# Seven products in both last MLP chunks, masks added by VectorE, and another order of the first loads

## The chip, the core and the metric

The kernel runs on one core of a Trainium2 chip. The metric is the device time of one execution in microseconds (us). Before the change the median of three runs is 2133.43 us (2133.31 to 2133.77). The trace that is read below is that of one more, profiled execution of the same kernel.

Engines by their names in the trace: PE is TensorE (PEld its weight loads), DVE is VectorE, ACT is ScalarE, POOL is GpSimd, SP is SyncE. SPq, ACTq and POOLq are the queues on which these issue DMAs. PSUM holds matmul results, SBUF everything else.

## The reference

Two decoder layers on x of 256 tokens by 2048 features, all in float32:

```python
for i in range(2):
    h = rms_norm(x, norm_mix[i])
    x = x + (nsa_mixer if i == 0 else gla_mixer)(h, ...)
    h = rms_norm(x, norm_mlp[i])
    x = x + jnp.square(jax.nn.relu(h @ w_up)) @ w_down      # 2048 -> 8192 -> 2048
```

`nsa_mixer` is attention with 16 query heads over 4 key groups and three branches (16 compressed keys, selected blocks, a window). With 256 tokens the selected blocks and the window cover all earlier keys, so two of the branches are causal attention over 256 keys. Scores that are not allowed are replaced by -1e30 before the softmax. `gla_mixer` is gated linear attention with 4 heads; the causal part within a sequence is computed by levels of halving blocks.

## The kernel before

**Arithmetic.** Each float32 operand of a large matmul is split into a high part of type fp32r (ACT casts it: tile `wh` for weights) and the rest (DVE subtracts: `wl`). A product is three matmuls: high by high, high by low, low by high. A matmul streams 512 columns against a 128x128 stationary tile. `a_half` consumes one weight half (128x1024: two k tiles of 512 columns) with 12 matmuls, six for each block `t` of 128 tokens.

**Stages in time.** NSA projections and attention (to about 270 us), NSA output projection (to 395), MLP of layer 0 (to about 1058), GLA (to about 1417 with its output projection after it), MLP of layer 1 (to the end).

**The MLP.** The hidden dimension is cut into 8 chunks of 1024. Chunk `c` computes hidden activations of `c + 1` (items `U`, 16 matmuls each) between the items of its own down product. In chunks 0 to 6 the down product of 256 tokens by 1024 hidden by 1024 output columns is done by a seven-product scheme (two groups a chunk, items `S`; a product is 12 matmuls of 512 columns). Sums of weight blocks that it needs are made by DVE or by accumulating DMAs on POOL's queue; sums of activation blocks (seven planes instead of four) by DVE in `hidden`. Chunk 7 (`SEVENS[7]` = 0) is plain: 16 items `C`, each one `a_half`.

**The order of the work** is written out by `Plan`: it adds up assumed costs for PE, ACT and DVE while the program is generated. Side work (attention heads, the GLA exponents, the norms) are generators, `streams`, that yield the time at which their next step is ready; `tick`, called every few matmuls, steps those that are ready. Engines then run their instruction lists in order. What a step is assumed to cost therefore decides where its instructions stand, not how long they take.

**Start.** SP issues the norm gains (`cid`, columns 128 on), then four quarters of the first two weight units, x's second pair of feature tiles, two halves, one unit of 1 MB, then x's third and fourth pair. ACT's queue loads x's first pair. Six idle products (12 entries in the trace) run on PE until data are there.

**GLA, first head.** `exponents` (four streams, one a head, one after the other) builds the decay factors: copies from `laT` and `rest`, additions, two tiles `g` of 8 levels a head. `attn` multiplies them with keys and queries (`g<-g,kq`), makes score blocks (`psx<-g`), transposes three of them (`psx<-cid,g`), places them with 20 predicated copies into `att` (line 1747), and splits `att` into `ath`. `head_out` multiplies `ath` with the values (`psx<-g,ath`).

**NSA scores.** `attend` (line 1331) makes the scores of one head in PSUM. The mask is added by a matmul of an identity with the mask (`maskr`, `identr`), twice a head; DVE takes row maxima (`reduce`), ACT exponentiates from PSUM.

Of the kernel before, what the change touches and what calls it, by code (L numbers as in the profile page):

```python
# [10 lines left out]
F32 = mybir.dt.float32  # L11
# [18 lines left out]
SEVENS = (2, 2, 2, 2, 2, 2, 2, 0)  # L30
# [3 lines left out]
class Plan:  # L34
# [49 lines left out]
    def spawn(self, gen):  # L84
        s = {"gen": gen, "ready": 0.0, "need": {}, "done": False}
        self.streams.append(s)
        self._step(s)
        return s
# [9 lines left out]
    def tick(self, slack=3200.0):  # L98
        taken = set()
        for s in list(self.streams):  # L100
# [8 lines left out]
    def drain(self, s, enough=lambda: False):  # L109
        while not s["done"] and not enough():  # L110
            before = [(id(q), q["ready"], q["need"]) for q in self.streams]
            self.tick(1e9)
# [3 lines left out]
    def wait(self, needs):  # L116

        while not all(sum(f < 1e12 for f in self.slots[tag]) >= n for tag, n in needs.items()):
            self.tick(1e9)
# [4 lines left out]
def trunk_kernel(ctx: ExitStack, tc: tile.TileContext, a: dict, out: bass.AP):  # L124
# [159 lines left out]
    nc.sync.dma_start(cid[:, P:], a["cid"][:, P:])  # L284
# [7 lines left out]
    nc.scalar.dma_start(xpair[0], a["x"][0])  # L292
    nc.gpsimd.memset(mhalf, -0.5)
# [62 lines left out]
    class Weights:  # L356
# [46 lines left out]
        def load_first(self, between):  # L403
# [4 lines left out]
            for j, (i, lo, hi) in enumerate(((0, 0, 512), (0, 512, 1024), (1, 0, 512), (1, 512, 1024), (0, 1024, 2048), (1, 1024, 2048))):  # L408
                nc.sync.dma_start(self.raws[i][:, lo:hi], self.units[i][0][:, lo:hi])  # L409
# [119 lines left out]
    MIXES = {0: "C" * 16, 2: "UU" + "SUSUSUSUSUUSUS" + "SUSUSUSUSUUSUS"}  # L529

    def mlp_items(c):
        return MIXES[SEVENS[c]]

    def mlp_units(layer):
# [8 lines left out]
        for c in range(8):  # L543
            down = a["mlp_down"][layer, c]
            n = {"U": 0, "S": 0, "C": 0}
            for it in mlp_items(c):
                i = n[it]
                n[it] += 1
                if it == "S":
                    if i % 7 == 0:  # L550
                        g = weights.group([down[i // 7, u] for u in range(4)])
# [5 lines left out]
                else:  # L557
                    if i % 2 == 0:
                        uc = weights.unit(down[SEVENS[c] + i // 8, i // 2 % 4])
# [184 lines left out]
    class PrepTokens(Prep):  # L744
# [3 lines left out]
        def start(self, b):  # L748
            if b == 0:
# [37 lines left out]
    def mlp(prep, after, last):  # L787
        op = prep.op
        with tc.tile_pool(name="mlpz", bufs=1) as zp:
# [20 lines left out]
            class Up:  # L810


                def __init__(self, c):
                    self.c = c
                    self.pairs = []
                    self.zz = None
                    self.pss = {}

                def half(self, f, half):
# [10 lines left out]
                    if f % 2 == 0:  # L830
                        self.pairs.append(pair_tile(c, f // 2))
                    last_z[:] = [W.spawn(self.hidden(ps, f))]

                def hidden(self, ps, f):
# [17 lines left out]
                    n = 7 if "S" in mlp_items(self.c) else 4  # L852
                    if n == 7:
                        both = pz[:, 0, :]
                        both = bass.AP(tensor=both.tensor, offset=both.offset,
                                       ap=[list(both.ap[0]), [3 * P, 2], [1, P]])
# [3 lines left out]
                    ht = self.pairs[f // 2][0]  # L860
# [18 lines left out]
            class Seven:  # L879
# [4 lines left out]
                def __init__(self, pairs, b):  # L884
# [4 lines left out]
                def product(self, name):  # L889
# [31 lines left out]
            class Plain:  # L921


                def __init__(self, c, pairs, first):
                    self.c, self.pairs, self.first = c, pairs, first
# [1079 lines left out]
```

## Time and profile before

| | |
|---|---|
| median of 3 runs | 2133.43 us |
| the profiled execution: its time, its span | 2133.26 us, 2131.5 us |
| TensorE clock granted, mean over the span | 0.999 of full speed |
| PE busy | 2121.5 us (100%), 10971 matmuls |
| DVE busy | 1784.3 us (84%) |
| ACT busy | 1358.4 us (64%) |
| DMA | 482.20 MB, mean 226 GB/s |

A busy time counts an instruction from its start to its modelled end. Matmuls overlap, so the mean duration of a 512 column matmul in the page (393 ns) is not its price; the distance from one start to the next is. A time in a timeline is the start, from the span's beginning; the number after it is the time that the merged instructions cover; in square brackets stands the idle time of the engine before them and what ended it.

### The profile page before, as it was taken

Reading aid. Unit: us, or ns where it says so; the run is one execution under the profiler, and the core shown is the slowest. Engines: PE = TensorE matmul, PEld = TensorE weight load, DVE = VectorE, ACT = ScalarE, POOL = GpSimd, SP = SyncE. Lnnn points to the kernel's source line nnn. Section 1 sums busy time; section 2 is a strip of 40 time slices with the busy share of each in tenths; the row PEclk is TensorE's granted clock in tenths of the full one; section 3 lists DMA queues with packets and bytes.
Section 4 is the critical chain, followed back from the end, with each engine's and each line's share of the span. In section 5 each row is a group of like instructions: output and inputs, shape, how many; then the busy total and the mean of one; then the engine's idle time right before and its main releaser. Section 6 shows DMA issues by size and latency. Waiting matters only on the chain.

```text
span 2131.5 us, 29821 instructions
## 1 busy us (share of the span) xinstructions
PE 2121.5 (100%) x10971; PEld 1797.3 (84%) x10971; DVE 1784.3 (84%) x2626; ACT 1358.4 (64%) x2047; POOL 154.9 (7%) x184
## 2 busy tenths in 40 slices
PE   9999999999999999999999999999999999999999
PEld 7888888888888888888888788888888888888887
DVE  7778777789999999998658987667899999999985
ACT  6568676666667666666566564536666666667663
POOL 0010100000110011001000000000000100010010
PEclk9999999999999999999999999999999999999999
DMA  7554444769889879878645354556698898798784
GB/s 287 205 198 139 153 164 149 235 227 297 257 241 299 265 243 281 274 240 244 203 162 194 130 176 173 174 187 238 225 300 258 238 291 268 244 279 278 240 240 153
DMA packets 97826, 482.20 MB, mean 226 GB/s; under 512 B 12176, under 2 KB 12832, under 8 KB 64144
## 3 DMA queue, kind: packets, MB, share of 16 engines
q1 hardware_dynamic: 76320, 403.53, 52.2%
q0 software_dynamic: 21216, 76.51, 18.0%
q8 instruction: 86, 1.41, 0.2%
q14 instruction: 60, 0.49, 0.1%
q10 hardware_dynamic: 144, 0.26, 0.0%
HBM read 404.76 MB, written 2.10 MB: 191 GB/s over the span
## 4 chain that ended last, share of the span: by engine, by line
PE 98%; DVE 1%; DMA 0%; issue 0%; ACT 0%; SPq 0%; ACTq 0%
PE psa L166 59%; PE psx L166 37%; PE psx L170 2%; DVE wl L201 0%; DVE g L201 0%; DMA raw<-in_nsa_in_dram 0%; DVE att L1747 0%; DVE g L1599 0%; DVE laT L201 0%; DVE rest L201 0%; DVE g L205 0%; ACT wh L197 0%; DVE xt L205 0%; DVE ath L201 0%; SPq L409 0%
## 5 line engine op out<-in xcount | busy, mean ns | idle before, releaser
L166 PE MATMUL psa<-wh,op 128*128 128x512 f32 x2616 | 849.7, 393 | 0.2 <-ACT wh L197 0.2
L201 DVE TENSOR_TENSOR wl<-raw,wh 128x1024 fp32r<-128x1024 f32 (+1 forms) x530 | 643.1, 1218 | 182.3 <-ACT wh L197 171.3
L197 ACT CAST wh<-raw 128x1024 fp32r<-128x1024 f32 (+1 forms) x534 | 557.5, 1046 | 291.8 <-PE psa L166 260.5
L166 PEld LDWEIGHTS psa<-wh,op 128*128 128x128 f32 x2616 | 492.4, 188 | 102.6 <-ACT wh L197 0.6
L201 DVE TENSOR_TENSOR wl<-sraw,wh 128x1024 fp32r<-128x1024 f32 x392 | 473.5, 1220 | 52.4 <-ACT wh L197 47.3
L166 PE MATMUL psx<-op,wh 128*128 128x512 f32 (+1 forms) x2080 | 515.8, 390 | 0.0
L166 PE MATMUL psa<-wl,op 128*128 128x512 f32 x1308 | 511.2, 391 | 0.2 <-DVE wl L201 0.2
L197 ACT CAST wh<-sraw 128x1024 fp32r<-128x1024 f32 x392 | 412.2, 1053 | 152.4 <-PE psa L166 59.5
L166 PEld LDWEIGHTS psx<-op,wh 128*128 128x128 f32 (+1 forms) x2080 | 385.1, 188 | 77.8
L166 PE MATMUL psa<-wh,ht 128*128 128x512 f32 x1128 | 382.0, 391 | 0.0
L166 PEld LDWEIGHTS psx<-op,wl 128*128 128x128 f32 x2048 | 279.5, 191 | 20.0
L166 PEld LDWEIGHTS psa<-wl,op 128*128 128x128 f32 x1308 | 246.3, 188 | 48.5 <-DVE wl L201 0.8
L166 PE MATMUL psx<-op,wl 128*128 128x256 f32 x2048 | 286.2, 283 | 0.0
L166 PEld LDWEIGHTS psa<-wh,ht 128*128 128x128 f32 x1128 | 212.8, 189 | 39.0
L166 PE MATMUL psa<-wl,ht 128*128 128x512 f32 x564 | 221.7, 393 | 0.0
L338 POOL DMA_DIRECT2D sraw<-sraw x140 | 119.8, 920 | 1289.5 <-DVE pz L201 429.9
L205 DVE SCALAR_TENSOR_TENSOR xt<-psa,r,xt 128x512 f32<-128x512 f32 x212 | 157.4, 745 | 26.9 <-PE psa L166 26.1
L197 ACT COPY zz<-psx 128x256 f32<-128x256 f32 x128 | 47.6, 372 | 169.0 <-PE psx L166 168.8
L166 PEld LDWEIGHTS psa<-wl,ht 128*128 128x128 f32 x564 | 106.7, 189 | 15.3 <-DVE wl L201 0.4
L201 DVE TENSOR_TENSOR sraw<-sraw,sraw 128x1024 f32<-128x1024 f32 x84 | 102.6, 1221 | 1.0
L201 DVE TENSOR_TENSOR zz<-psx,zz 128x256 f32<-128x256 f32 x128 | 53.7, 419 | 13.6 <-ACT zz L197 13.6
L197 ACT CAST ht<-pz 128x896 fp32r<-128x896 f32 (+1 forms) x40 | 37.1, 928 | 14.6 <-DVE pz L205 13.5
(195 smaller groups left out, 1195.8 us busy)
## 6 DMA issues: line engine op xcount, KB each, us to landing
raw<-in_mlp_up_dram SPq DMA_DIRECT2D x128, 1024.0 KB, 7.5
sraw<-in_mlp_down_dram SPq DMA_DIRECT2D x224, 512.0 KB, 11.4
sraw<-sraw POOLq DMA_DIRECT2D x140, 512.0 KB, 9.5
raw<-in_gla_in_dram SPq DMA_DIRECT2D x48, 1024.0 KB, 4.9
raw<-in_nsa_in_dram SPq DMA_DIRECT2D x38, 1024.0 KB, 4.8
raw<-in_nsa_out_dram SPq DMA_DIRECT2D x16, 1024.0 KB, 4.8
raw<-in_mlp_down_dram SPq DMA_DIRECT2D x16, 1024.0 KB, 4.9
raw<-in_gla_out_dram SPq DMA_DIRECT2D x16, 1024.0 KB, 4.8
```

The lines of the kernel that those rows point to most:

```text
L166: nc.tensor.matmul(dst, lhsT, rhs, skip_group_check=True, **kw)
L170: nc.tensor.transpose(dst, src, idn)
L197: nc.scalar.copy(dst, src)
L201: nc.vector.tensor_tensor(dst, x, y, op=op)
L205: nc.vector.scalar_tensor_tensor(dst, x, s, y, op0=op0, op1=op1)
L338: nc.gpsimd.dma_start(dst, src, accum_op=ALU.add)
```

## The change

Five things are edited.

1. `SEVENS` becomes a table for both layers, with 1 for chunk 7: half of its output columns (blocks 2 and 3) by seven products, half (blocks 0 and 1) plain, in the order `CCSCSCSCSCSCSCS`. Plain products need a plane that the seven-product planes overwrite, so `hidden` first stores it apart (`over`). Block results are finished by `finished`: output DMA in layer 1, the start of the next norm (`after.start`) in layer 0.
2. The masks leave PE. DVE adds them while it takes the maxima (`least`, one fused instruction with a second one that reads out its accumulator), writes the masked scores to SBUF, and ACT exponentiates from there.
3. First loads: the gains go to ACT's queue behind x's first pair; SP starts with the weights; x's third pair goes ahead of the 1 MB unit. The first two units lie contiguous in DRAM by piece.
4. `Plan`: the streams `exponents` are marked `later`, stepped after all others and not beyond the slack while another is drained.
5. `Plan`: assumed costs; a GLA copy of 128 elements is reckoned by another, lower formula (`vcopy` in place of `keep`), a predicated copy by 235 in place of 110.

```diff
-SEVENS = (2, 2, 2, 2, 2, 2, 2, 0)
+SEVENS = ((2, 2, 2, 2, 2, 2, 2, 1), (2, 2, 2, 2, 2, 2, 2, 1))
...
-    def tick(self, slack=3200.0):
+    def tick(self, slack=3200.0, later=True):
         taken = set()
-        for s in list(self.streams):
+        for s in sorted(self.streams, key=lambda s: s["later"]):
+            if s["later"] and not later:
+                return
...
+    def least(dst, x, y, acc):
+
+        W.run("dve", free(dst) * 1.042 + 150, [dst, acc], [x, y])
+        nc.vector.tensor_tensor_reduce(dst, x, y, scale=-1.0, scalar=3e38, op0=ALU.add, op1=ALU.min, accum_out=acc)
...
-    nc.sync.dma_start(cid[:, P:], a["cid"][:, P:])
...
     nc.scalar.dma_start(xpair[0], a["x"][0])
+    nc.scalar.dma_start(cid[:, P:], a["cid"][:, P:])
...
-                nc.sync.dma_start(self.raws[i][:, lo:hi], self.units[i][0][:, lo:hi])
+
+                flat = self.units[i][0].rearrange("p n -> (p n)")
+                nc.sync.dma_start(self.raws[i][:, lo:hi], flat[P * lo:P * hi].rearrange("(p c) -> p c", p=P))
...
+    MIXES = {0: "C" * 16, 1: "CCSCSCSCSCSCSCS", 2: "UU" + "SUSUSUSUSUUSUS" + "SUSUSUSUSUUSUS"}
...
                     if i % 7 == 0:
-                        g = weights.group([down[i // 7, u] for u in range(4)])
+                        g = weights.group([down[2 - SEVENS[layer][c] + i // 7, u] for u in range(4)])
+                        if c == 7:
+                            g.odd = 1
...
+                    ht, over = self.pairs[f // 2][0], self.over[f // 2] if self.over else None
+                    if over is not None:
+
+                        copy(over[:, 0, :], pz[:, 1, :])
+                        yield W.ready(over)
+                        tt(over[:, 1, :], pz[:, 1, :], over[:, 0, :].bitcast(F32), ALU.subtract)
...
+                        if self.c == 7 and name in ("b21", "t2", "d2", "t4"):
+                            finished(t, b + k)
...
+            def finished(t, b):
+                if last:
+                    nc.sync.dma_start(out[t * P:(t + 1) * P, b * 512:(b + 1) * 512], xt[t][b])
+                elif t == 1:
+                    after.start(b)
...
-                    if mask is not None:
-                        mm(dst, cst["identr"], mask, start=False, stop=False)
...
-                largest(nb0[:, 0:1], s0[:, 256:272])
-                largest(nb0[:, 1:3], s0[:, 0:256].rearrange("p (b k) -> p b k", b=2))
+                masked(nb0[:, 0:1], 0, s0[:, 256:272], mask[:, 272:288])
+                for b in range(2):
+                    masked(nb0[:, 1 + b:2 + b], 32 + b * P, s0[:, b * P:(b + 1) * P], mask[:, 16:16 + P])
+                W.give(s0, W.t["dve"])
...
-                        keep(second, uv[:, :, 1, :])
+                        vcopy(second, uv[:, :, 1, :])
...
-                        W.run("dve", 110.0, [att], [pl])
+                        W.run("dve", 235.0, [att], [pl])
...
-                        sums = sums + [W.spawn(exponents(hd, sums[-1], es[hd]))]
+                        sums = sums + [W.spawn(exponents(hd, sums[-1], es[hd]), True)]
...
     weights.load_first(lambda j: load_x(({}, {0: 3900.0}, {}, {1: 8300.0}, {}, {})[j]))
+    load_x({2: 11200.0})
     weights.load()
-    load_x({2: 13000.0, 3: 13700.0})
+    load_x({3: 13700.0})
```

Three places in the instruction lists. The first is ACT's list at the start. `xs` are x's pairs (the one that has the lowest number came first), `raw_107` and `raw_108` the first two weight units, `raw_116` or `raw_117` the third. Before:

```order
L193 ACTIVATE op_142<-xs_88,cid 128x256 x2
L197 CAST wh_172<-raw_107 128x1024
L197 CAST wh_186<-raw_108 128x1024
L193 ACTIVATE op_197<-xs_89,cid 128x256 x2
L193 ACTIVATE op_197<-xs_90,cid 128x256 x2
L193 ACTIVATE psx_209<-xs_87 128x256
L197 CAST wh_217<-raw_116 128x1024
```

After:

```order
L198 ACTIVATE op_142<-xs_87,cid 128x256 x2
L202 CAST wh_172<-raw_107 128x1024
L198 ACTIVATE op_178<-xs_88,cid 128x256 x2
L202 CAST wh_190<-raw_108 128x1024
L198 ACTIVATE op_178<-xs_89,cid 128x256 x2
L198 ACTIVATE psx_211<-xs_86 128x256
L202 CAST wh_218<-raw_117 128x1024
```

The third pair (`xs_89`, now `xs_88`) is scaled one weight cast earlier; on DVE its first remainder now stands directly ahead of the remainder of `wh_172` (`wl_173`), where it stood behind two of these.

The second place is DVE's list in GLA, from the remainder of the first head's `ath` to the first multiplications of the second head (`g<-g,kq`). Before:

```order
L201 TENSOR_TENSOR wl_11391<-raw_11189,wh_11390 128x1024
L201 TENSOR_TENSOR ath_11405<-att_11113,ath_11405 128x384
L205 SCALAR_TENSOR_TENSOR g_2058_11411<-g_2058_11411,psa_11130 128x512
L205 SCALAR_TENSOR_TENSOR g_2058_11411<-g_2058_11411,psa_11131 128x512
L201 TENSOR_TENSOR g_2001_10890<-g_2001_10890,kq_10126 128x256 x4
L1611 MEMSET rest_10123 128x256
```

After:

```order
L206 TENSOR_TENSOR wl_11291<-raw_11096,wh_11290 128x1024
L221 COPY g_2040_11176<-laT 128x128
L221 COPY g_2040_11176<-rest_10149 128x128
L206 TENSOR_TENSOR laT<-g_2040_11176,laT 128x4x32
L206 TENSOR_TENSOR rest_10149<-g_2040_11176 128x4x32
L206 TENSOR_TENSOR ath_11311<-att_11067,ath_11311 128x384
L206 TENSOR_TENSOR wl_11318<-raw_11096,wh_11317 128x1024
L221 COPY g_2040_11176<-laT 128x128
L221 COPY g_2040_11176<-rest_10149 128x128
L206 TENSOR_TENSOR laT<-g_2040_11176,laT 128x2x64
```

The second head's multiplications stood three rows behind `ath`; now they begin 20 rows behind it. On PE 24 matmuls of weights stood between the first head's `psx<-g,ath` and the second head's score blocks, and now 75 do; between the transposes for `att` and `psx<-g,ath` there were 42 and now are 66.

The third place is DVE's list at the first attention head. `psx` are scores in PSUM, `p` the tile that is exponentiated, `nb` the negated maxima. Before:

```order
L201 TENSOR_TENSOR wl_1611<-raw_1466,wh_1610 128x1024
L220 TENSOR_REDUCE nb_305_1636<-psx_1629 128x1
L220 TENSOR_REDUCE nb_305_1636<-psx_1629 128x2
L220 TENSOR_REDUCE nb_311_1648<-psx_1641 128x1
L220 TENSOR_REDUCE nb_311_1648<-psx_1641 128x2
L212 TENSOR_SCALAR f_1568<-f_1568,r2d 128x4 x2
```

After:

```order
L206 TENSOR_TENSOR wl_1571<-raw_1413,wh_1570 128x1024
L230 ISA p_1595,nb_294_1600<-psx_1594,mask 128x16
L230 ISA nb_294_1600 128x1
L230 ISA p_1595,nb_294_1600<-psx_1594,mask 128x128
L230 ISA nb_294_1600 128x1
L230 ISA p_1595,nb_294_1600<-psx_1594,mask 128x128
```

Two reductions of the first score block of a head become three fused instructions, each with a read-out. Over all 16 heads 64 reductions go and 96 fused instructions come (32 of 16 columns, 64 of 128 columns).

## Rows read from the trace of the kernel before

**Rows 1.** The page's part 1: busy us (share of span) x instructions.

```profile
PE 2121.5 (100%) x10971; PEld 1797.3 (84%) x10971; DVE 1784.3 (84%) x2626; ACT 1358.4 (64%) x2047; POOL 154.9 (7%) x184
```

**Rows 2.** Chain of waits in order of time: start, us, what; plain chunk 7, layer 0.

```profile
1030.84 10.90 PE psa L166 x48
```

**Rows 3.** Timeline of PE inside one head's scores.

```profile
185.65 0.29 PE L166 MATMUL psx<-maskr,identr 128*128 128x272 f32 x1
185.78 0.29 PE L166 MATMUL psx<-kT,qT 128*128 128x272 f32 x1
```

**Rows 4.** Timeline of all engines, first 15 us.

```profile
0.74 0.39 SPq L284 DMA_DIRECT2D cid<-in_cid_dram  x1
...
1.19 1.84 SPq L409 DMA_DIRECT2D raw<-in_nsa_in_dram  x4
...
8.12 0.50 PE L166 MATMUL psa<-wl,op 128*128 128x512 f32 x1 [0.22 <-DVE wl L201]
...
11.16 1.06 ACT L197 CAST wh<-raw 128x1024 fp32r<-128x1024 f32 x1 [0.20 <-DMA raw<-in_nsa_in_dram]
...
13.04 0.39 PE L166 MATMUL psa<-wl,op 128*128 128x512 f32 x1
...
14.23 1.71 ACT L193 ACTIVATE op<-xs,cid 128x256 fp32r<-128x256 f32 x4 [2.02 <-DMA xs<-in_x_dram]
```

**Rows 5.** Timeline of PE in GLA, first and second head.

```profile
1196.44 0.58 PE L170 MATMUL psx<-cid,g 128*128 128x128 f32 x3
...
1206.61 0.62 PE L166 MATMUL psx<-g,ath 128*128 128x512 f32 x2
1209.95 2.44 PE L166 MATMUL psx<-g,ath 128*128 128x512 f32 x7 [2.73 <-DVE ath L201]
...
1214.89 0.39 PE L166 MATMUL psa<-wl,op 128*128 128x512 f32 x1
...
1220.98 1.65 PE L166 MATMUL psx<-g 128*32 128x64 f32 x68 [0.64 <-DVE g L201]
...
1223.98 0.33 PE L170 MATMUL psx<-cid,g 128*128 128x128 f32 x1 [0.46 <-DVE g L205]
1224.64 0.55 PE L170 MATMUL psx<-cid,g 128*128 128x128 f32 x3 [0.33 <-DVE g L205]
```

**Rows 6.** Windows: stretch, us, busy us of each engine, granted clock (PEclk), DMA share.

```profile
1210.00:1215.00 5.00, 5.00 (x15) 3.97 (x16) 4.96 (x21) 1.38 (x4) 0.00 (x0) 0.66 0.31 131
...
160.00:340.00 180.00, 180.00 (x962) 153.88 (x961) 138.29 (x337) 135.86 (x463) 13.60 (x12) 1.00 0.44 152
```

**Rows 7.** Tile `att`, 1195 to 1210 us: ns min/median/max, first and last start.

```profile
L1747 DVE COPY_PREDICATED att<-lmask,psx x20: 176/199/234, 1198.9 to 1203.4; 64x32 f32<-64x32 uint8 x20
```

**Rows 8.** Timeline of DVE in GLA, first head's end.

```profile
1206.12 1.23 DVE L201 TENSOR_TENSOR wl<-raw,wh 128x1024 fp32r<-128x1024 f32 x1
1207.26 0.23 DVE L1599 COPY g<-laT 128x128 f32<-128x128 f32 x1
...
1207.93 0.23 DVE L1599 COPY g<-laT 128x128 f32<-128x128 f32 x1
...
1209.34 0.56 DVE L201 TENSOR_TENSOR ath<-att,ath 128x384 fp32r<-128x384 f32 x1
1209.93 1.28 DVE L205 SCALAR_TENSOR_TENSOR g<-g,psa 128x512 f32<-128x512 f32 x2
1211.13 1.43 DVE L201 TENSOR_TENSOR g<-g,kq 128x256 f32<-128x256 f32 x4
```

**Rows 9.** Groups by line, DVE, 160 to 340 us: form, count, busy us, mean ns, idle before.

```profile
L220 DVE TENSOR_REDUCE mx<-psx 128x2 f32<-128x256 f32 x32 | 11.9, 414 | 0.0
L220 DVE TENSOR_REDUCE nb<-psx 128x1 f32<-128x16 f32 x32 | 5.4, 170 | 12.9 <-PE psx L166 12.9
```

**Rows 10.** Timeline of DVE: the fused multiply-and-sum that GLA uses.

```profile
1122.73 0.42 DVE L1661 CUSTOM_DVE_ANT_0 dj<-g,g 128x256 f32<-128x256 f32 x1
...
1123.19 0.43 DVE L1661 CUSTOM_DVE_ANT_0 dj<-g,g 128x256 f32<-128x256 f32 x1
```

More of the change, by code (lines that the diff above doesn't have):

```diff
@@ L545, in mlp_units @@
             n = {"U": 0, "S": 0, "C": 0}
-            for it in mlp_items(c):
+            for it in mlp_items(layer, c):
                 i = n[it]
@@ L558, in mlp_units @@
                     if i % 2 == 0:
-                        uc = weights.unit(down[SEVENS[c] + i // 8, i // 2 % 4])
+                        uc = weights.unit(down[i // 8, i // 2 % 4])
                     weights.half(uc, i % 2)
@@ L788, in mlp @@
         op = prep.op
+        layer = int(last)
+        sevens = SEVENS[layer]
         with tc.tile_pool(name="mlpz", bufs=1) as zp:
@@ L815, in __init__ @@
                     self.pairs = []
+                    self.over = []
                     self.zz = None
@@ L943, in half @@
                         W.give(self.ps[t], W.t["dve"])
-                    if self.c < 7:
-                        return
-                    if last:
+                    if self.c == 7:
                         for t in range(NT):
-                            nc.sync.dma_start(out[t * P:(t + 1) * P, b * 512:(b + 1) * 512], xt[t][b])
-                    if after is not None:
-                        after.start(b)
+                            finished(t, b)
+            def finished(t, b):
[3 more added lines that the diff above has]
+                    after.start(b)
             last_z = []
@@ L965, in mlp @@
             for c in range(8):
-                items = mlp_items(c)
+                items = mlp_items(layer, c)
                 nxt = Up(c + 1) if c < 7 else None
-                plain = Plain(c, cur.pairs, 2 * SEVENS[c])
+                plain = Plain(c, cur)
                 n = {"U": 0, "S": 0, "C": 0}
@@ L980, in mlp @@
                         if i % 7 == 0:
-                            seven = Seven(cur.pairs, 2 * (i // 7))
+                            seven = Seven(c, cur.pairs, 2 * (2 - sevens[c] + i // 7))
                         seven.product(Group.ORDER[i % 7])
@@ L1337, in attend, with score @@
                 p = ptile([P, 800])
-                def score(ps, lo, n, t, mask):
+                def score(ps, lo, n, t):
                     qh = qT[:, 0, t * P:(t + 1) * P]
@@ L1378, in attend @@
                 largest(mx[:, 0, :], s1a[:, 0:256].rearrange("p (b k) -> p b k", b=2))
-                largest(mx[:, 1, :], s1b[:, 16:272].rearrange("p (b k) -> p b k", b=2))
+                for b in range(2):
+                    masked(mx[:, 1, b:b + 1], 544 + b * P, s1b[:, 16 + b * P:16 + (b + 1) * P], mask[:, 16:16 + P])
+                W.give(s1b, W.t["dve"])
                 tt(nb1[:, 1:3], mx[:, 0, :], mx[:, 1, :], ALU.min)
                 yield W.ready(nb1)
-                ex(16, s1b[:, 0:16], nb1, 0, 3)
@@ L1595, in decays @@
                 yield W.ready(laT)
-            def keep(dst, src):
-                W.run("dve", free(dst) * 1.042 + 75, [dst], [src])
-                nc.vector.tensor_copy(dst, src)
             def exponents(hd, wait, e):
@@ L1897, in _units_down, with _pieces @@
     u = plain.copy()
-    for c, n in enumerate(SEVENS):
-        u[:, c, :n] = seven[:, c, :n]
+    for layer in range(2):
+        for c, n in enumerate(SEVENS[layer]):
+            u[layer, c, 2 - n:] = seven[layer, c, 2 - n:]
+    return u
+def _pieces(u):
+    u = u.copy()
+    for b in range(2):
+        u[b, 0] = np.concatenate([u[b, 0, :, lo:hi].ravel() for lo, hi in ((0, 512), (512, 1024), (1024, 2048))]).reshape(P, 2048)
     return u
```

102 lines of the change are left out of this document (56 added, 46 removed).

## The prediction

> **What bounds the kernel now.** I read page part 1 first: PE is busy 2121.5 us of a span of 2131.5 us, DVE 1784.3, ACT 1358.4 [rows 1]. So time goes only where PE gets fewer columns, where it waits, or where its clock falls. Then the chain of waits: it runs through PE nearly everywhere, and its steps give PE's price per matmul. 48 matmuls of 512 columns take 10.90 us in one unbroken step, 0.227 us each [rows 2]. Inside one head's scores two matmuls of 272 columns start 0.13 us apart [rows 3]. Last come the places where PE waits for another engine: the first 15 us [rows 4] and GLA's first two heads, where PE waits for DVE [rows 5] and the granted clock drops to 0.66 in one stretch of 5 us [rows 6], between the levels 1.2 and 2.4 GHz.
>
> **The change part by part.** The sum is made against the profiled execution, 2133.26 us, which lies 0.17 us under the median of the runs, 2133.43.
>
> *Seven products in chunk 7.* Each layer's last chunk goes from 16 items of 12 matmuls (192) to 180, so 24 matmuls of 512 columns go: 24 x 0.227 = **-5.5 us** [rows 2]. Chunk 7 is then what chunks 0 to 6 already are on half of its columns; DVE adds 12 weight remainders of 1024 columns and some block sums over both layers, POOL 12 accumulating DMAs. Their price is nothing while they land before their matmuls. What hides them is PE's own weight matmuls: one item of 12 lasts 2.7 us, a weight remainder 1.14 (1206.12 to 1207.26, [rows 8]). If that cover fails, PE waits; this is a rival below.
>
> *Masks leave PE.* 32 mask matmuls at 0.13 = **-4.0 us** [rows 3], if their ends stay hidden.
>
> On DVE 32 reductions of 256 columns (0.414 each, half of these maxima of another form at about the same price) and 32 of 16 columns (0.170) go [rows 9]: 32 x 0.414 + 32 x 0.170 = 18.7 us. In come 32 fused instructions of 16 columns and 64 of 128, with read-outs. No row shows this operation. From below the nearest row is the narrow reduction, 0.17 us; from above the fused multiply-and-sum of 256 columns with its read-out, 0.46 us from one start to the next [rows 10]. I take 0.33 for 128 columns, between the two and nearer the latter since it too is fused, reads two operands and is read out, and 0.21 for 16. That is 64 x 0.33 + 32 x 0.21 = 27.8 us, so DVE gets 9 us more (16.3 - 18.7 = -2.4 at 0.17, 44.2 - 18.7 = +25.5 at 0.46). Between 160 and 340 us DVE is busy 138.3 of 180 us [rows 6], so 41.7 us of idle time hide it. In that stretch PE does not stand still (busy 180.0), because the heads are laid between weight matmuls. A maximum is three instructions and their read-outs later than two reductions; ACT's exponentials wait for it, and the value product behind these on PE has weight matmuls ahead of it as before. ACT's exponentials change only their source, at no cost that I can bound from a row: with ACT busy 135.9 of 180 us, also under cover.
>
> *First loads.* The gains leave SP's queue, so the weights are issued at 0.74 instead of 1.19, 0.45 us earlier [rows 4]. The remainder that PE got at 8.12 can come up to 0.45 us earlier; that is the lower end, -0.45. Against it, x's third pair moves ahead of a 1 MB unit and on DVE its remainder stands ahead of `wl_173`. Half a unit had landed at 11.16, and by 14.23 that 1 MB and 256 KB of x had: 3.07 / 5 = 0.61 us per 256 KB [rows 4]. So the third pair lands at about 11.16 + 0.61 - 0.45 = 11.3. Then ACT scales (0.45), DVE subtracts (0.4), and `wl_173` takes 1.2: 13.4. PE wanted that remainder at 13.04 [rows 4]. I take **+0.35**, range -0.45 to +0.8.
>
> The gains themselves now stand behind x's first pair on ACT's queue, which ACT needs with it; PE does its idle products until the weights are there, so this hides.
>
> The Trainium skill ("DMA: Bandwidth & Descriptors", section "Issuing engines are not separate DMA queues") says that DMAs started by different engines run on the same 16 DMA engines and interleave, so that starting them elsewhere saves only the time of issue. The issue times of [rows 4] agree (0.45 us between the two issues on SP); a forecast by queues alone would make the gain larger, the page leaves only the 0.45.
>
> *GLA.* Here PE loses time before. `psx<-g,ath` starts with two matmuls at 1206.61, whose third should follow 0.45 us later and starts at 1209.95, behind DVE's `ath`: 2.9 us lost. After it the clock is 0.66 [rows 6], and 14 matmuls from 1209.95 to 1214.89 take 4.94 us in place of 14 x 0.227 = 3.18: 1.76 lost. Then waits of 0.64, 0.46 and 0.33 [rows 5]. Together **6.1 us**.
>
> DVE's path from the transposes at 1196.44 to `ath`'s end at 1209.9 was 13.5 us: four weight remainders of 1.14, 20 predicated copies of 0.237 (4.5 us over 19 steps, [rows 7]), `ath` 0.57, and six exponent levels of 0.67 each less two instructions (1207.26 to 1207.93, [rows 8]). PE's cover was 42 weight matmuls, 9.5 us. After, the cover is 66, 15.0 us; by the order of the instructions DVE has four remainders, the 20 copies, two exponent levels, two fused operations of 0.60 each (1209.93 to 1211.13, [rows 8]) and `ath`: 4.6 + 4.7 + 1.3 + 1.2 + 0.6 = 12.4. Nothing is waited for at `ath`, and with the wait the slow clock goes.
>
> What is late next is the second head's scores. Before they were held by the last multiplications at 1220.98 [rows 5]. After, DVE has between `ath` and the last of these: six remainders (6.8), 16 multiplications of 0.36 (5.7, [rows 8]), 33 small exponent and norm instructions at about 0.17 (5.5) and about 4.4 of other work, 22.4 us in all. PE has 75 weight matmuls, nine of values and eight transposes: 84 x 0.227 + 0.9 = 20.0, then 40 score matmuls of the first block that need less. DVE also starts up to 2.6 us ahead of PE (15.0 - 12.4). So the two arrive together within a microsecond. I leave 0.6 us: **-5.5**. The ends are -7 (the waits there cost a little more than I counted) and 0 (they only move).
>
> The Trainium skill ("TensorE: Matmul & The Clock Gate", Part 1) says that an idle array is throttled to half its clock and has to earn full speed again. The trace agrees for the wait of 2.73 us, followed by 0.66, while no fall shows behind those of 0.64, 0.46 and 0.33. Were every remaining wait to bring the slow clock, each would cost 1.8 us more.
>
> *New small waits* in attention (later maxima), at the norm after chunk 7 (its blocks are now finished two at a time in another order) and at the stored plane in `hidden`: I take **+0.4**, range 0 to +3.
>
> Sum: -5.5 - 4.0 + 0.35 - 5.5 + 0.4 = -14.25; 2133.26 - 14.25 = 2119.0, and 0.17 for the median: **2119.2 us**.
>
> **Rivals.**
>
> *The GLA waits only move.* DVE does the same exponents, copies and multiplications as before, so if it, not the order, bounds the stretch, PE waits at the second head's scores for what it no longer waits for at `ath`. For it: the 22.4 against 20.0 us above. Against: before, 42 and 24 weight matmuls covered the two waits, now 66 and 75, and after the second head no wait of such size stands in the trace. Then -5.5 - 4.0 + 0.35 + 0.4 = -8.75: **2124.7**.
>
> *Slower: DVE becomes the bound of the attention stage.* One mechanism: the fused instruction with its read-out is dear. DVE has 41.7 us free and 18.7 us of reductions leave, so 60.4 / 96 = 0.63 us apiece is the point from which it decides. At 0.8 us (nearly twice the dearest row) it takes 76.8 us, 16.4 more than there is room for; with the maxima then late at every head, about 1 us for 16 heads more, PE waits some 32 us, and less the 14.25 - 0.4 of the rest the time is about 2133.3 - 13.9 + 32 = **2151**; 2142 at 0.7. Against: [rows 10] has 0.46 for twice the columns.
>
> *Chunk 7 runs into late sums.* Accumulating DMAs land just behind the casts that need them, in both layers, because only one of its two groups is of seven products: 5 to 10 us come back, **2124 to 2129**. Against: chunks 0 to 6 run twice as many groups without a wait in the trace.
>
> *All hides.* First loads gain their 0.45, the GLA stretch 7, nothing new is waited for: -5.5 - 4.0 - 0.45 - 7.0 = -17: **2116.5**.
>
> **How the numbers follow.** The forecast has 0.62, own range 2115.5 to 2122; waits that move 0.22; late sums 0.06; all hides 0.06; slower 0.04. The range of 8 in 10 takes in the forecast's, that of moved waits, and part of the late sums: 2115.5 to 2126. What a measurement of this kernel can tell from no change is about 0.2%, 4.3 us. Of the cases, the first two and all-hides lie more than that below, late sums partly: faster 0.92, same 0.04, slower 0.04.
>
> **What would show it.** PE's row count falls by 56. In the chain, chunk 7 is unbroken and 2.7 us shorter in each layer. The masks go from PE's timeline and the fused instructions' mean on DVE lies between 0.17 and 0.46 us. `psx<-g,ath` has no idle time before it, no stretch near 1210 has a granted clock under 0.9, and waits before the second head's scores stay under 1 us. The `wl` of the first unit's second half comes at about 13.4. I am wrong if a wait of over 2 us stands in GLA (first rival), on maxima at every head (second), or before `C` and `S` items of chunk 7 (third).

## The result and the profile after

The changed kernel takes 2118.65 us (median of 6 runs, 2118.44 to 2119.84) against 2133.48 us (2133.31 to 2133.9): a ratio of 0.9931, 95% interval 0.9919 to 0.9944. Forecast were 2119.2 us with 2115.5 to 2126.0. Its profiled execution is the slowest of the six, 2119.84 us; why is told below.

Part 1 of its page (busy us, share, instructions), beside [rows 1]:

```profile
PE 2110.3 (100%) x10915; PEld 1787.0 (84%) x10915; DVE 1818.0 (86%) x2807; ACT 1377.6 (65%) x2067; POOL 159.4 (8%) x196
```

PE has 56 matmuls fewer, as forecast (24 + 32). DVE is busy 34 us longer, and PE waits for little of that (the section on why the prediction was right ends with the waits).

The profiled executions differ by 13.42 us (2133.26 - 2119.84). Where it went is read by following single PE instructions through both traces: how much earlier the same instruction starts.

| up to | before | after | gained since the row above |
|---|---|---|---|
| 101st weight matmul (the expectations below call it the 100th) | 30.23 | 31.25 | -1.02 |
| first `psx<-op,wl` (MLP, layer 0, first products) | 393.71 | 390.76 | 3.97 |
| first down product of layer 0 | 443.03 | 440.07 | 0.01 |
| first down product of layer 1 (chunk 7 of layer 0 and GLA lie between) | 1509.48 | 1498.27 | 8.25 |
| last matmul (chunk 7 of layer 1) | 2126.91 | 2113.13 | 2.57 |
| end of the profiled execution | 2133.26 | 2119.84 | -0.36 |

Masks 3.97; chunk 7 of layer 0 at 12 x 0.227 = 2.72 leaves 5.53 for GLA; chunk 7 of layer 1 2.57; the start costs 1.02 in this execution. The split of the 8.25 us is worked out here, and e5 below, which has the planner of before, bears it out: from the first down product of layer 0 to that of layer 1 it takes 1063.79 us, against 1066.45 before and 1058.20 after, so 2.66 for chunk 7 and 5.59 for GLA. These are the terms of the sum: 4.0, 2.7, 5.5, 2.7, and a start that was put at 0.35.

The places, in the trace of the changed kernel. First PE in GLA, first and second head (timeline; start, us covered, in brackets the wait and what ended it), which answers to [rows 5]:

```profile
1189.39 2.21 PE L171 MATMUL psx<-g,ath 128*128 128x512 f32 x9
...
1209.41 3.25 PE L171 MATMUL psx<-g 128*128 128x128 f32 x108
...
1216.96 0.64 PE L175 MATMUL psx<-cid,g 128*128 128x128 f32 x3 [0.69 <-ACT g L202]
```

The nine `psx<-g,ath` run in one piece, where they stood 2.73 us; the 108 score matmuls of the second head run in one piece too. What is late next is something else: the transposes wait 0.69 us for ACT's copy of the small score blocks. The windows show the clock (last but two columns: granted clock, DMA share, GB/s), to be held against the first of [rows 6]:

```profile
1186.00:1191.00 5.00, 5.00 (x24) 4.14 (x23) 4.96 (x18) 1.75 (x3) 0.00 (x0) 1.00 0.77 277
...
1212.00:1217.00 5.00, 4.31 (x44) 3.24 (x32) 4.96 (x13) 3.53 (x12) 0.00 (x0) 1.00 0.55 193
```

Full clock in the stretch of `ath`, where no wait stands; it stays full behind the 0.69 us too, since matmuls of 512 columns follow each other there after 0.23 us.

The fused instruction, in DVE's timeline at one head's second score block. Its price is the distance from start to start:

```profile
336.44 0.17 DVE L230 CUSTOM_DVE_ANT_0 p<-psx,mask 128x16 f32<-128x16 f32 x1
336.53 0.08 DVE L230 DVE_READ_ACCUMULATOR2_ANT nb<- 128x1 f32 x1
336.53 0.28 DVE L230 CUSTOM_DVE_ANT_0 p<-psx,mask 128x128 f32<-128x128 f32 x1
336.74 0.08 DVE L230 DVE_READ_ACCUMULATOR2_ANT nb<- 128x1 f32 x1
336.74 0.29 DVE L230 CUSTOM_DVE_ANT_0 p<-psx,mask 128x128 f32<-128x128 f32 x1
```

0.21 us for 128 columns and 0.09 for 16, read-out included, because the read-out lies beside the next one. The window 160 to 340 us, the second of [rows 6]:

```profile
160.00:340.00 180.00, 179.90 (x944) 152.89 (x943) 139.99 (x457) 138.41 (x461) 12.32 (x12) 1.00 0.44 152
```

DVE's busy time rises by 1.7 us there, not 9.

The start (all engines, first 15 us), beside [rows 4]:

```profile
0.74 1.81 SPq L421 DMA_DIRECT2D raw<-in_nsa_in_dram  x4
...
5.37 0.91 ACT L198 ACTIVATE op<-xs,cid 128x256 fp32r<-128x256 f32 x2 [2.23 <-DMA cid<-in_cid_dram]
...
6.84 0.58 PE L171 MATMUL psa<-wh,op 128*128 128x512 f32 x1 [0.16 <-ACT wh L202]
...
11.89 0.91 ACT L198 ACTIVATE op<-xs,cid 128x256 fp32r<-128x256 f32 x2 [0.81 <-DMA xs<-in_x_dram]
...
14.11 0.50 PE L171 MATMUL psa<-wl,op 128*128 128x512 f32 x1 [0.78 <-DVE wl L206]
```

The weights are issued at 0.74 as forecast, but ACT's first scaling, at 3.56 before, waits for the gains until 5.37, and the weight remainder that was reckoned for 13.4 comes at 14.11.

### The profile page after: what moved, and what is told of

Same layout as the page of the kernel before. It is cut to its first block, busy times and chain, and to the rows that moved or that the text cites. A ratio compares the mean times of both kernels' runs of the same rounds, so it can differ in the third digit from the quotient of the medians.

```text
span 2118.1 us, 29981 instructions
## 1 busy us (share of the span) xinstructions
PE 2110.3 (100%) x10915; PEld 1787.0 (84%) x10915; DVE 1818.0 (86%) x2807; ACT 1377.6 (65%) x2067; POOL 159.4 (8%) x196
## 4 chain that ended last, share of the span: by engine, by line
PE 97%; DVE 1%; DMA 1%; ACT 0%; issue 0%; SPq 0%; DVEq 0%; ACTq 0%
PE psa L171 59%; PE psx L171 37%; PE psx L175 2%; DMA xs<-in_x_dram 1%; DVE wl L206 0%; DVE g L206 0%; ACT wh L202 0%; DVE g L210 0%; ACT p L198 0%; DVE g L221 0%; DVE op L210 0%; DVE xt L210 0%; DVE xt L206 0%; ACT att L202 0%; DVE rest L206 0%
## 5 line engine op out<-in xcount | busy, mean ns | idle before, releaser
L206 DVE TENSOR_TENSOR wl<-raw,wh 128x1024 fp32r<-128x1024 f32 (+1 forms) x514 | 623.3, 1216 | 152.9 <-ACT wh L202 139.3
L202 ACT CAST wh<-raw 128x1024 fp32r<-128x1024 f32 (+2 forms) x518 | 540.5, 1045 | 250.6 <-PE psa L171 225.3
L206 DVE TENSOR_TENSOR wl<-sraw,wh 128x1024 fp32r<-128x1024 f32 x420 | 507.3, 1218 | 45.1 <-ACT wh L202 41.8
L202 ACT CAST wh<-sraw 128x1024 fp32r<-128x1024 f32 x420 | 442.0, 1053 | 155.8 <-PE psa L171 75.6
L348 POOL DMA_DIRECT2D sraw<-sraw x152 | 130.5, 944 | 1362.6 <-DVE pz L206 468.4
L210 DVE SCALAR_TENSOR_TENSOR xt<-psa,r,xt 128x512 f32<-128x512 f32 x218 | 162.0, 744 | 21.4 <-PE psa L171 20.6
L171 PEld LDWEIGHTS psa<-wl,ht 128*128 128x128 f32 x558 | 105.5, 189 | 14.8
L206 DVE TENSOR_TENSOR sraw<-sraw,sraw 128x1024 f32<-128x1024 f32 x88 | 107.4, 1220 | 1.0
L202 ACT CAST ht<-pz 128x896 fp32r<-128x896 f32 x40 | 37.8, 944 | 15.9 <-DVE pz L210 14.9
```

The source lines that it names most:

```text
L171: nc.tensor.matmul(dst, lhsT, rhs, skip_group_check=True, **kw)
L202: nc.scalar.copy(dst, src)
L206: nc.vector.tensor_tensor(dst, x, y, op=op)
L210: nc.vector.scalar_tensor_tensor(dst, x, s, y, op0=op0, op1=op1)
L348: nc.gpsimd.dma_start(dst, src, accum_op=ALU.add)
```

## Experiments

The question in each: which edit gives which part, and what of the reasons holds. "After" is the changed kernel. Dots in a diff stand for lines left out. Each median is of 4 to 11 runs; each trace is of one of them.

### The start

Four kernels move only the first loads of after.

e1, all of edit 3 undone:

```diff
+    nc.sync.dma_start(cid[:, P:], a["cid"][:, P:])
...
-    nc.scalar.dma_start(cid[:, P:], a["cid"][:, P:])
...
-                nc.sync.dma_start(self.raws[i][:, lo:hi], flat[P * lo:P * hi].rearrange("(p c) -> p c", p=P))
+                nc.sync.dma_start(self.raws[i][:, lo:hi], self.units[i][0][:, lo:hi])
...
-    load_x({2: 11200.0})
     weights.load()
-    load_x({3: 13700.0})
+    load_x({2: 13000.0, 3: 13700.0})
```

> The changed kernel with the first loads as in the kernel before (gains first in SyncE's queue, x's third pair behind the 1 MB unit, the first units not cut into contiguous pieces). Theory: in the profiled execution of the changed kernel PE starts on weights at 6.84 us instead of 6.12 and waits 0.78 us at 14.11, because the gains on ScalarE's queue land at 5.37; with the loads back this start is as before (first weight matmul at 6.1, no wait at 13 to 14) and the profiled time falls by the 1.02 us that the 100th weight matmul is late: 2119.84 - 1.02 = 2118.8; if the timed runs of the changed kernel carry the same loss, the median is 2118.65 - 1.0 = 2117.6. Rival: the late gains are an accident of that one execution (its time is 1.2 us above the median of the others); then the start is no worse than before in the other runs and the median stays at 2118.6 within 0.3, or rises to 2119.0 if the earlier weights gain 0.45.

e2, only the first two edits of this diff (gains first on SP, ahead of the weights; the units stay contiguous by piece):

> The changed kernel with only the gains back as the first load of SyncE's queue; x's third pair stays ahead of the 1 MB unit. Theory (late gains cause it): ACT's first scaling starts at about 3.6 us as before, the first weight matmul at 6.1, and most of the 1.02 us is back; what is left at 13 to 14 us is the third pair alone, 0.3 us. Median 2117.9 if the timed runs carry the loss. Rival (third pair causes it): PE still waits about 0.8 us for the weight remainder at 13 to 14 us and the median stays at 2118.6.

e3, gains on ACT's queue, the two lines swapped:

```diff
+    nc.scalar.dma_start(cid[:, P:], a["cid"][:, P:])
     nc.scalar.dma_start(xpair[0], a["x"][0])
-    nc.scalar.dma_start(cid[:, P:], a["cid"][:, P:])
```

> The changed kernel with the gains still on ScalarE's queue but ahead of x's first pair there. Theory (the gains are late because of their place behind x's pair, while SyncE's weights take the transfers): gains and pair land at about 3.6 to 4.2 us, ACT scales at 4.2 at the latest, and the weights keep their 0.45 us, so the first weight matmul comes between 5.7 and 6.3 and the median falls to 2117.6 to 2118.2. Rival (small rows of the gains are slow on whatever place once weights are being loaded): ACT still waits until about 5 us, and the median stays at 2118.6.

e4, only the last part (x's third pair behind the unit):

> The changed kernel with only x's third pair back behind the 1 MB unit; the gains stay on ScalarE's queue. Theory (late gains): the first weight matmul is still at 6.8 in the profiled execution and the wait at 14.11 goes, since DVE no longer has the pair's remainder ahead of the weight remainder; the 100th weight matmul is late by 0.7 instead of 1.02. Rival (third pair causes the loss): the start is as before, and the median is 2117.6.

Measured:

| kernel | median us (range) | ACT's first scaling | first weight matmul | 101st | profiled us |
|---|---|---|---|---|---|
| after | 2118.65 (2118.44 to 2119.84) | 5.37 | 6.84 | 31.25 | 2119.84 |
| e1 | 2118.55 (2117.94 to 2119.63) | 3.51 | 6.07 | 30.84 | 2119.63 |
| e2 | 2119.44 (2118.62 to 2120.68) | 3.55 | 5.45 | 32.55 | 2120.68 |
| e3 | 2118.62 (2118.07 to 2120.63) | 5.03 | 6.50 | 30.42 | 2118.62 |
| e4 | 2118.60 (2118.44 to 2119.86) | 5.52 | 6.99 | 30.29 | 2118.49 |

The rival of the first expectation holds: the 1.02 us are an accident of one execution. Kernels with after's own first loads passed the 101st weight matmul at 30.15 (e12), 30.27 (e6), 30.28 (e11), 30.30 (e5), 30.39 (e10), 31.25 (after) and 32.07 (e9); with the old loads it was 29.99 (e7), 30.23 (before and e8) and 30.84 (e1). The middle ones, 30.30 and 30.23, are the same. In the five rows above the profiled time less the 101st matmul is 2088.1 to 2088.8, so what makes these five profiled executions differ by up to 2.2 us lies in the start. The runs of one kernel, which scatter by about 1 to 3 us, have one trace among them; that theirs is the same cause is likely, not shown.

The theory of late gains is right about the wait and wrong about its price. e3 misses in another way: there the gains land in time, and ACT waits until 5.03 for x's pair, which now comes second. In each profile that has them on ACT's queue behind x's pair ACT starts on them at 5.4 to 5.7, and PE starts 0.7 to 1 us later than before; but the weights then lie ahead, and the losses that e1 has at 12 and 18 us (0.5 and 0.7 us) are absent in e4. e2, with an early start, is the slowest by the median (its range overlaps the others'), outside both of its expectations: in its profiled execution PE starts on weights at 5.45 and then stands 1.82 us.

PE in e2 (timeline), and the windows of the same stretch:

```profile
13.80 0.50 PE L171 MATMUL psa<-wl,op 128*128 128x512 f32 x1 [1.82 <-DVE wl L206]
```

```profile
15.00:18.50 3.50, 3.50 (x10) 2.68 (x10) 2.71 (x5) 3.50 (x8) 0.00 (x0) 0.51 0.86 335
```

The granted clock behind that wait is 0.51, the lower of the two levels, 1.2 GHz; eight matmuls take 0.2 us more each, 1.6 us. In this execution an early start into a wait cost more than a late start without one. The start at 5.45 is not e2's alone: with the old loads PE's first weight matmul comes anywhere from 5.29 (e8) to 6.12 (before). The pieces' contiguous layout was not undone by itself.

### The parts by themselves

e5 leaves out edits 4 and 5, so the planner is the one of before:

```diff
-    def tick(self, slack=3200.0, later=True):
+    def tick(self, slack=3200.0):
...
-                        vcopy(second, uv[:, :, 1, :])
+                        keep(second, uv[:, :, 1, :])
...
-                        W.run("dve", 235.0, [att], [pl])
+                        W.run("dve", 110.0, [att], [pl])
```

> The changed kernel with the planner as before: the exponents' streams not stepped last, the assumed costs of a GLA copy and a predicated copy as before. Theory (the order in GLA gave 5.5 us): PE waits 2 to 3 us for the first head's ath again, the granted clock falls behind it, and the median is 2118.65 + 5.5 = 2124.2. Rival (part of the 5.7 us in which the two traces differ between 1200 and 1300 us comes from the masks or chunk 7 having moved the instructions): 2119 to 2122.

e6 leaves out only edit 5 (the costs):

```diff
-                        vcopy(second, uv[:, :, 1, :])
+                        keep(second, uv[:, :, 1, :])
...
-                        W.run("dve", 235.0, [att], [pl])
+                        W.run("dve", 110.0, [att], [pl])
```

> The changed kernel with the streams stepped last, but the assumed costs of before. Theory (the order of the streams gives the gain, since it puts the 20 exponent instructions behind ath and more weight matmuls ahead of it): no wait of over 0.5 us before psx<-g,ath, median 2118.6 to 2119.5. Rival (the costs decide when attn's steps are taken to be ready, a predicated copy at 235 instead of 110 moves ath's values 2.5 us later on PE): a wait of 1 to 3 us at ath remains and the median is 2120.5 to 2124.

e12 leaves out only edit 4 (`later`):

```diff
-                        sums = sums + [W.spawn(exponents(hd, sums[-1], es[hd]), True)]
+                        sums = sums + [W.spawn(exponents(hd, sums[-1], es[hd]))]
```

> The changed kernel with the new assumed costs, but the exponents' streams not stepped last. The streams without the costs gave 2120.7, neither gives 2124.5, both give 2118.65. Theory (the order of the streams takes away the wait at ath, the costs only trim the two waits behind it by 2.1 us together): the wait of 2 to 3 us at ath is there, 2122 to 2124.5. Rival (the costs alone put ath far enough behind): no wait at ath, 2119 to 2121.

e7 is the kernel before with edit 2 alone:

```diff
-                    if mask is not None:
-                        mm(dst, cst["identr"], mask, start=False, stop=False)
...
+                    least(p[:, c0:c0 + n], src, m, dst)
```

> The kernel before with only the masks moved to DVE. Theory: 32 matmuls of 0.125 us go and DVE has room: 2133.4 - 4.0 = 2129.4. Rival (the maxima that come later are waited for): 2130 to 2135. Its GLA keeps the wait at ath.

e8 is the kernel before with edit 1 alone:

```diff
-SEVENS = (2, 2, 2, 2, 2, 2, 2, 0)
+SEVENS = ((2, 2, 2, 2, 2, 2, 2, 1), (2, 2, 2, 2, 2, 2, 2, 1))
```

> The kernel before with only the seven products in both last chunks. Theory: 24 matmuls of 0.227 us go and no sum is late: 2133.4 - 5.5 = 2127.9. Rival (the accumulating DMAs or the reordered norm of GLA cost something that the whole change hides): 2128.5 to 2131.

Measured: e5 2124.48 us (expected 2124.2), e7 2129.30 (2129.4), e8 2127.95 (2127.9). So the planner's edits are worth 5.8 us at the end of after, the masks 4.2 and chunk 7 5.5 at the start of before; 5.8 + 4.2 + 5.5 = 15.5 against 14.8 measured together. The traces, from which the starts can be left out, add up better: from the 101st weight matmul to the end of the span e7 gains 4.27 on before and e8 4.66, and after gains 5.58 on e5, 14.5 together, where after gains 14.41 on before.

The rival of e8 (the reordered norm costs something that the whole change hides) holds in a small part. Its GLA is 0.5 us longer than before (319.84 us in place of 319.32 from the first score matmul to the first down product of layer 1), with a longer wait at the second head's scores, where before had 0.6:

```profile
PE psx L166 <- DVE g L201: 2.2, 1, 2.2
```

e6 2120.74 and e12 2126.22 tell the planner's two edits apart. Waits of PE over the whole span (us in total, times, longest), e5:

```profile
PE psx L166 <- DVE ath L201: 2.7, 1, 2.7
...
PE psx L170 <- DVE g L205: 0.8, 2, 0.5
PE psx L166 <- DVE g L201: 0.6, 1, 0.6
```

e6:

```profile
PE psx L175 <- ACT g L202: 1.4, 1, 1.4
PE psx L171 <- DVE g L206: 1.3, 1, 1.3
```

e12:

```profile
PE psx L170 <- DVE g L205: 6.8, 1, 6.8
```

With the streams last (e6) the wait for `ath` is gone, as the theory says, and two waits of 1.3 to 1.4 us remain at the second head, so that the median falls into the rival's range. The costs trim these. Without the order (e12) the wait for `ath` is gone too, against the theory, but the time lies outside both ranges: one wait of 6.8 us stands at the transposes of the first head's output. In DVE's list 14 copies and additions of the exponents and eight multiplications of the second head stand ahead of what these need (1204.04 to 1209.09 us). That a cheaper copy lets the planner put them there is argued from its rule, not tried apart from the costs. Behind this wait the clock is half:

```profile
1210.00:1213.00 3.00, 2.70 (x8) 2.14 (x9) 3.00 (x7) 0.84 (x2) 0.00 (x0) 0.50 0.01 3
```

Edits 4 and 5 give -3.7 and +1.7 alone and -5.8 together (from 2124.48), so neither has a price of its own.

### DVE's room in attention

e10 and e11 issue each fused instruction twice and four times; the orders on PE and ACT are unchanged. e10:

```diff
         nc.vector.tensor_tensor_reduce(dst, x, y, scale=-1.0, scalar=3e38, op0=ALU.add, op1=ALU.min, accum_out=acc)
+        nc.vector.tensor_tensor_reduce(dst, x, y, scale=-1.0, scalar=3e38, op0=ALU.add, op1=ALU.min, accum_out=acc)
```

> The changed kernel with each fused mask-and-maximum instruction issued twice (96 more, the second gives the same values); orders on PE and ACT unchanged. The trace of the changed kernel has 0.211 us from one to the next for 128 columns and 0.094 for 16, so DVE gets 64 x 0.211 + 32 x 0.094 = 16.5 us more, against 40 us idle in 160 to 340 us. Theory (cover holds to a mean price of about 0.6 us per fused instruction): 2118.65, at most 1 us more. Rival (what counts is that the maxima come late, not the room): about 1 us a head, 2122 to 2135.

> The same with each fused instruction four times: 49.5 us more on DVE, a mean of 0.69 us for what is one fused instruction in the changed kernel, beyond the point (0.57 to 0.63 us) from which the prediction let DVE bound the attention stage. Theory: DVE lacks about 10 us of room there, so 2118.65 + 10 = 2128 to 2135. Rival (DVE's lag is taken up later, by the idle time behind the attention stage, or PE waits nowhere for maxima): 2118.6 to 2122.

e10 takes 2126.23 us, e11 2174.77: 7.6 and 56 us more. The added work was more than both expectations reckoned, because a second instruction that writes the same columns follows after 0.33 us in place of 0.21 (see the last section): from start to start all fused instructions take about 18 us in after, 46 in e10 and 103 in e11, so 28 us came in where 16.5 were expected, and 85 where 49.5 were. In e10 the theory of room falls all the same, since 28 us are less than the 40 us idle, and its time lies in the rival's range (the maxima come late). In e11 85 us are about 45 more than the room; with the larger amount the theory of room gives some 2163, and the measured 2174.77 does not tell a lack of room and lateness apart. The window 160 to 340 us, e10 and e11:

```profile
160.00:340.00 180.00, 175.96 (x909) 147.57 (x908) 156.02 (x614) 134.71 (x448) 12.17 (x12) 1.00 0.45 153
```

```profile
160.00:340.00 180.00, 153.86 (x733) 124.62 (x732) 162.46 (x776) 112.28 (x363) 12.28 (x12) 0.95 0.38 129
```

In e10 DVE still has 24 us of idle time there and PE stands 4 us. PE's waits between 155 and 380 us in e10:

```profile
PE psx L171 <- DVE nb L230: 1.2, 1, 1.2
PE psx L171 <- DVE mx L231: 0.9, 1, 0.9
PE psx L171 <- DVE pT L206: 0.5, 1, 0.5
PE psx L175 <- DVE mx L231: 0.4, 1, 0.4
```

In after this view lists no wait of PE between 155 and 380 us. The first two of e10 are score matmuls (`psx`) that wait for the fused instruction of an earlier score block, `nb` and `mx`. By the program DVE must have read a PSUM tile before the next scores go into it (`W.give(s0, W.t["dve"])` frees it behind the fused instructions). So it is DVE's time in that chain that counts here, not its room; a kernel with more such tiles was not tried. e11, with the clock at 0.95, has waits of the same kinds, up to 4.5 us. Per place (one fused instruction in after) e10 spends 46 / 96 = 0.48 us and after 18 / 96 = 0.19.

### A better version

e9 adds one edit to after: ACT's copy that the transposes at 1216.96 wait for goes ahead of seven copies.

```diff
-                yield W.ready(pa)
+                yield W.ready(pq)
...
+                copy(at[:, 0:2, :], pq[:, 0:2, :])
+                copy(at[0:64, 2, :], pq[0:64, 2, :])
+                W.give(pq, W.t["act"])
                 copy(att[:, 2, :], pa[:, 2 * P:3 * P])
...
-                yield W.ready(pq)
...
-                copy(at[:, 0:2, :], pq[:, 0:2, :])
-                copy(at[0:64, 2, :], pq[0:64, 2, :])
-                W.give(pq, W.t["act"])
```

> The changed kernel with one more edit in attn: ACT copies the small score blocks to g (what PE transposes) before it copies the seven pieces of att, not after. In the trace of the changed kernel PE waits 0.69 us at 1216.96 for that copy, which stands behind 1.21 us of att copies on ACT. Theory (ACT's order makes that wait): it goes, 2118.65 - 0.85 = 2117.8. Rival (the wait is DVE's or the cast's ahead, or the transposes are also called earlier on PE): it stays within 0.3 us of 2118.65.

2117.81 us (2117.64 to 2120.42), as the theory had it; ratio to before 0.9929 (0.9917 to 0.9942), an interval that overlaps after's. The order on ACT in its trace, and the transposes behind:

```profile
1217.00 0.52 ACT L202 COPY g<-psx 128x256 f32<-128x256 f32 x2
...
1217.42 1.25 ACT L202 COPY att<-psx 128x128 f32<-128x128 f32 x7
1217.42 0.64 PE L175 MATMUL psx<-cid,g 128*128 128x128 f32 x3
```

The transposes come right behind the copy, with 0.28 us over their usual distance left, where after had 0.85. That the wait is shortened is shown, and what it is worth too: from GLA's first score matmul to the first down product of layer 1 e9 takes 330.05 us, where after, e1 to e4, e10 and e11, whose GLA is the same, take 330.75 to 330.85, so 0.7 us. That the whole kernel gained 0.8 us cannot be told from the scatter: its profiled execution took 2120.42, with the start of 32.07 and one loss of 0.8 us at a weight remainder in layer 0's MLP (569.12 us) that after does not have.

## Why the prediction was right

- *Seven products.* -5.5 forecast; e8 gives -5.5, the traces -2.57 in layer 1. The wait on late sums (third rival) is not there: chunk 7 of both layers is one chain of PE in the trace of after. A piece of it in layer 0, and its end in layer 1, in after and before:

```profile
1033.33 18.39 PE psa L171 x81
```

```profile
2069.97 43.56 PE psa L171 x192
```

```profile
2081.03 46.28 PE psa L166 x204
```

  192 matmuls without a break at 0.227 each, where 204 stood, 2.72 us less; then the last sum and the output as before. In the table the layer gains 2.57, since after has one small wait more in its MLP, and 0.36 are given back behind the last matmul.
- *Masks.* -4.0 forecast; -3.97 in the traces, -4.2 in e7. DVE's price of the fused instruction was mis-sized: 0.33 was taken for 128 columns and 0.21 for 16, measured are 0.21 and 0.09. The step that failed is the choice of a price "nearer the latter", which is [rows 10] with 256 columns at 0.46. That row was too dear besides: from the second of its two instructions to the next, which writes another tile, it is 0.36 (see the last section). And the reductions were priced by their durations (0.414, 0.170, [rows 9]), while start to start they cost 0.33 and 0.085: in the trace of before two pairs of them take 0.82 us, up to the next instruction.

```profile
186.74 0.91 DVE L220 TENSOR_REDUCE nb<-psx 128x1 f32<-128x16 f32 x4
187.56 0.68 DVE L201 TENSOR_TENSOR p<-p,wg 128x512 f32<-128x512 f32 x1
```

  So DVE got 16.5 - 13.3 = 3.2 us more to do where 9 were reckoned. At 3.2 it cost PE 0.27 us at one place; at 9 it was not tried.
- *The slower rival* had a wrong point. "0.63 us apiece" came from idle time over a stretch of 180 us. e10 shows 7.6 us of loss at 0.48 us apiece, close to [rows 10], the upper bound of 0.46, at which the prediction's own step ("41.7 us of idle time hide it") would still have found nothing. That step was wrong; the forecast was right here because the instruction is cheap, not because DVE has room. In the rival's sum the rest is 14.25 + 0.4 = 14.65, not 13.85 (the 0.4 of waits is a loss); 0.8 us, which changes nothing.
- *First loads.* +0.35 forecast; about 0.1 measured by the medians (e1 against after), within a scatter of 1 to 2 us. The step "the gains ... so this hides" failed: ACT waited 2.23 us for them, and PE's first weight matmul came 0.72 later. What stood in its place: fewer waits behind the start, as the weights run ahead (by the distances from start to start 1.1 us are lost between 6 and 8 us before, 1.7 in e1 up to 19 us, 0.6 in e4). The 0.45 us earlier issue is there and gives nothing. The Trainium skill's section that the prediction quotes ("DMA: Bandwidth & Descriptors", "Issuing engines are not separate DMA queues") leaves nothing but the time of issue to be had from another queue. The runs agree in that no gain shows; but that ACT gets the gains at 5.4 in place of 3.6 is no matter of issue (they were issued at 1.18 instead of 0.74).
- *GLA.* -5.5 forecast; 5.53 in the traces, 5.8 in e5. The rival that the waits only move is refuted by the rows above: nothing is waited for at `ath`, and little at the scores. A remainder of 0.6 was left for the second head's scores; 0.85 is lost, at the transposes behind ACT, and 0.43 in two steps of the scores. The count of DVE's instructions was right (12.6 us from the first weight remainder behind the transposes to the end of `ath`, 12.4 forecast), the place of the next wait was not: ACT, on which the exponent's `ACTIVATE` and seven copies stand ahead, was left out of the count. That the term came out at 5.5 is in part luck. The loss before was taken from the idle times (6.1); from start to start the three waits behind `ath` and one step of the scores cost 2.2 us more than their usual distances, not 1.4, so 6.9 were lost, and 1.3 are left, not 0.6. Both sizes are short by 0.7 or 0.8 us and cancel.
- *New small waits.* 0.4 forecast. Found are 0.27 at 338.39 (next scores behind DVE's `pT`), 0.28 once in the MLP of layer 1, and 0.36 behind the last matmul, 0.9 in all.
- *The sum.* The median was forecast to 0.55 us, which is less than the 1.4 us by which the six runs of after differ. The traces support the large terms; that the total comes so near is also luck, since the start (by the medians 0.25 too dear) and the new waits (0.5 too cheap) miss in opposite directions.

## What to carry to other kernels

Count what stands between a producer and its consumer on every engine of the chain, not the idle share of one engine over a stage: in e10 a stage with 24 us of idle time on DVE lost 7.6 us to lateness. Two edits of a planner are one edit: run both alone before giving either a price. Where executions of one kernel differ by 1 to 2 us, look at the first 30 us of each before explaining the median of a small edit.

## What was not expected

The fused add-and-minimum with its read-out costs 0.21 us for 128 columns; two of them, 0.42, do the adding and the maxima for which a reduction of 256 columns alone takes 0.33. Two in a row that write different columns of `p` stand 0.21 us apart (336.53 and 336.74 above); where they write the same columns (e11) it is 0.33; the reason was not tried.

```profile
163.54 0.29 DVE L231 CUSTOM_DVE_ANT_0 p<-psx,mask 128x128 f32<-128x128 f32 x1
...
163.88 0.29 DVE L232 CUSTOM_DVE_ANT_0 p<-psx,mask 128x128 f32<-128x128 f32 x1
```

The 0.46 us of [rows 10] hold such a pair: both write `dj`, of which the program has one buffer. The second, at 1123.19, is followed by an instruction that writes another tile, 0.36 us later:

```profile
1123.55 1.22 DVE L201 TENSOR_TENSOR wl<-raw,wh 128x1024 fp32r<-128x1024 f32 x1
```

Small first loads are late in company. With the gains first on SP, x's pair and the gains land at 3.5 and 3.2 us (e1), before the weights, which are issued from 1.19 on. With the weights issued at 0.74 beside them, x's pair lands at 4.5 and the gains, behind it, at 5.3 (after); with the order swapped the gains land at 3.8 and the pair at 4.9 (e3). What is issued second on ACT's queue, at 1.18, is then the last of the two that ACT needs, whichever it is. It is not the cut into contiguous pieces: e2 has it, with the gains first on SP, and there they land at 3.5 and 3.2. Which shared resource does it was not tried.
